# Layer A's gate as g (1 + tanh(g/2)) at its eviction, and two moves in the order of work

## The chip, the core and the metric

The kernel runs on one core of one Trainium2 chip. The metric is device time in microseconds for one execution; times before are of three runs. The engines in the profile are PE (TensorE matmuls; PEld its weight loads), DVE (VectorE), ACT (ScalarE), POOL (GpSimd) and SP (SyncE, whose queue issues all of the transfers here).

## The reference, cut to what matters

A decoder trunk of two layers on 2048 tokens of width 1024, in float32. Layer A makes q, k, v, forget logits and a gate from one normalized input, runs causal attention with a forget bias, multiplies by the gate's SiLU and projects. Layer B has its own gate and a windowed attention over shared keys that get a partial rotary.

```
u = rmsnorm(h, norm_a_g)
q, k, v, f_logit, gate = split(u @ w_in_a)
o = fox_attention(rmsnorm(q), rmsnorm(k), v, log_sigmoid(f_logit + b))   # exp(...) / sum
h = h + (o * silu(gate)) @ w_out_a
k_shared = partial_rope(rmsnorm((rmsnorm(h) @ w_kv)[:, :256]), positions)
...                                                                      # layer B
```

Since silu(g) = g sigmoid(g) = g (1 + tanh(g/2)) / 2, the gate can be carried without the half if something else is halved.

## The kernel before, in words

All large products are done as three float32r matmuls of split operands (high x high, high x low, low x high), 128 x 128 weights against 512 columns. The stages, by the profiled execution's clock:

- *Layer A's projections* (0 to 605 us): tokens in 16 blocks; `vectors` loads the small gain vectors in the first group, through `load_vectors` on SP's queue. `constants` makes `fold`, a 128 x 32 matrix of ones that sums partial rows.
- *Layer A's attention* (`attention_a`, 605 to about 1475 us): 320 steps, 20 for each of 16 heads. A step makes two blocks of scores in the three "sc" banks (L801, L802, masks L805), takes their exponential on ScalarE (L810, L814) into a tile of the tag "st" (four buffers), rounds it (L815, ScalarE), takes the low part (L816, GpSimd), adds it to the running sum in the one "ac" bank (L827, VectorE; started by L819, ended by the reduction L715), and multiplies by v three steps later (L842, "pa" bank, evicted by L850 into "sq"). Row maxima of queries 13 steps ahead run in the "mx" banks (L753; L764 and L769 on VectorE) and are stored as rows by small transfers (L430). `recips` sums the partial sums through `fold` (L724), takes the reciprocal (L729) and stores it to `rd`.
- *The gate in between.* `gate` is a generator that yields once per matmul (L872); `feed(n)` draws from it up to a total of n. The gate has 4 x 8 tiles of 128 rows x 512 tokens, 24 matmuls each. Each tile gathers in the one "pb" bank and reads its weights in two loads of 512 KB into "wr" (two buffers, L868); it is copied by ScalarE (L878) into "sq" and stored to `gt` (L879). `feed` is called at the end of each step, so that 28 of the 32 tiles (768 less `KEPT` = 96 matmuls) are spread over the 320 steps, 2.1 matmuls per step; the last four follow while the output weights are split (`half`, L360 and L361, through `between`).
- At step 125 `silus` loads the first 512 tokens' gate (all 1024 rows), takes Silu in two ScalarE instructions (L939) and stores it back. For these tokens `gated` (L1026 to L1032) runs at the end of attention, without Silu of its own.
- *Output projection* (`out_a`, about 1512 to 1695 us): four times 512 tokens. While one is multiplied (L1070), `gated_load` and `gated` prepare the next: attention's two parts are added (GpSimd, L1026), Silu of the gate (ScalarE, L1028), times 1/sum (L1029), times gate (L1030), split (L1031, L1032).
- *Layer B*, to the end. `rotary` (L277 to L280) makes four small products of the cosines and sines with the key gain `gk16`; they depend on that gain's load and on the buffer "rot", which the attention's mask holds until its last row maximum.

The order of instructions on each engine is not the program's order alone: a planner places each instruction by its own estimate of when operands and buffers are ready, and each engine then works through its list strictly in order. `keep_in_program_order` pins an instruction behind the one traced before it on its engine.

Of the kernel before, what the change touches and what calls it, by code (L numbers as in the profile page):

```python
# [3 lines left out]

# [1 line left out]

# [6 lines left out]
F32R = mybir.dt.float32r  # L13
BF16 = mybir.dt.bfloat16
I32 = mybir.dt.int32
AF = mybir.ActivationFunctionType
ALU = mybir.AluOpType
# [4 lines left out]
P = 128  # L22
# [3 lines left out]
NDT = D // P  # L26
# [17 lines left out]
PREP_AT = (284, 293, 304, 309, 314)  # L44

RAW_AT = 302

SILU_AT = 6 * 20 + 5

KEPT = 4 * 3 * NDT  # L50

# [37 lines left out]
class Trunk:  # L89
# [55 lines left out]
    def constants(self):  # L145
        nc, cp, a = self.nc, self.const, self.a

        def select(view, src, pattern, base, cm, fill):
            nc.gpsimd.affine_select(
                out=view, in_=src, pattern=pattern, compare_op=ALU.is_ge,  # L150
                fill=fill, base=base, channel_multiplier=cm,
            )

        def tile_(name, shape, dt=F32):
            return cp.tile(shape, dt, name=name, tag=name)

        self.ones = tile_("ones", [P, P])
        nc.gpsimd.memset(self.ones, 1.0)
        self.tri = tile_("tri", [P, P])
        select(self.tri, self.ones, [[1, P]], 0, -1, 0.0)  # L160
        self.ident = tile_("ident", [P, P])
        select(self.ident, self.tri, [[-1, P]], 0, 1, 0.0)

        self.fold = tile_("fold", [P, 32])
        nc.vector.tensor_tensor(self.fold, self.ident[:, :32], self.ident[:, 32:64], ALU.add)
        for c in (64, 96):
            nc.vector.tensor_tensor(self.fold, self.fold, self.ident[:, c : c + 32], ALU.add)
        self.identb = tile_("identb", [P, P], BF16)
        nc.vector.tensor_copy(self.identb, self.ident)

        self.mask_s = tile_("mask_s", [P, 2 * P], BF16)
        nc.gpsimd.memset(self.mask_s[:, :P], NEG)
        nc.gpsimd.memset(self.mask_s[:, P:], 0.0)
        select(self.mask_s[:, P:], self.mask_s[:, P:], [[1, P]], 0, -1, NEG)

        self.band = tile_("band", [P, 2, P], BF16)
        nc.gpsimd.memset(self.band, 0.0)
        select(self.band[:, 0, :], self.band[:, 0, :], [[1, P]], -1, -1, NEG)
        select(self.band[:, 1, :], self.band[:, 1, :], [[-1, P]], 0, 1, NEG)

        self.loads = []
        warm = tile_("warm", [P, 1])
        nc.scalar.activation(warm, self.ones[:, :1], AF.Sqrt)

        def vector(name, n, views):
            t = tile_(name, [P, n])
            for rows, src in views:
                self.loads.append((t[rows], src))
            return t

        def column(name, src, n):
            return vector(name, n, [(slice(0, P), src.rearrange("(t p) -> p t", p=P))])

        def pair_column(name, src):
            col = src.rearrange("(p o) -> p o", o=1)
            return vector(name, 1, [(slice(0, HD), col), (slice(HD, P), col)])

        def row(name, src, n):
            return vector(name, n, [(slice(0, P), src.to_broadcast([P, n]))])

        self.g_a = column("g_a", a["norm_a_g"][0], NDT)
        self.bf = row("bf", a["b_forget"], H)
        self.g_qa = pair_column("g_qa", a["qnorm_a_g"][0])
        self.g_ka = pair_column("g_ka", a["knorm_a_g"][0])
        self.g_b = column("g_b", a["norm_b_g"][0], NDT)
        self.g_kv = column("g_kv", a["kv_norm_g"], NDT)
        self.g_qb = pair_column("g_qb", a["qnorm_b_g"][0])
        self.g_kb = pair_column("g_kb", a["knorm_b_g"])
        self.sink = row("sink", a["sinks"], H)
        self.gq16 = row("gq16", a["qnorm_b_g"][:, :ROT], ROT)  # L210
        self.gk16 = row("gk16", a["knorm_b_g"].rearrange("(o d) -> o d", o=1)[:, :ROT], ROT)
        self.nsink = tile_("nsink", [P, H])

    def load_vectors(self, loads):
# [454 lines left out]
    def attention_a(self, w_out, result):  # L669
# [184 lines left out]

        def gate():

            for ch in range(NCH):
                us = []
                for dt in range(NDT):
                    us.append([self.sb(t, [P, CH], F32R) for t in ("wh", "wl")])  # L860
                    for k in range(2):
                        nc.sync.dma_start(out=f_(us[dt][k]), in_=d["ut"][ch, k, dt])
                for ft in range(NDT):
                    ps = self.ps("pb", [P, CH])
                    for dt in range(NDT):
                        if dt % 4 == 0:
                            w = self.sb("wr", [P, 2, 2, 2, P], F32R)
                            nc.sync.dma_start(  # L868
                                out=f_(w), in_=d["wg"][ft, :, dt // 2 : dt // 2 + 2]
                            )  # L870
                        for i, (wk, uk) in enumerate(((0, 0), (0, 1), (1, 0))):
                            nc.tensor.matmul(  # L872
                                ps, w[:, dt // 2 % 2, wk, dt % 2, :], us[dt][uk],
                                start=(dt == 0 and i == 0), stop=(dt == NDT - 1 and i == 2),
                            )
                            yield
                    g = self.sb("sq", [P, CH])
                    nc.scalar.copy(g, ps)  # L878
                    nc.sync.dma_start(  # L879
                        out=d["gt"][ft * P : (ft + 1) * P, ch * CH : (ch + 1) * CH], in_=g  # L880
                    )

        pieces, done, loaded = [], 0, 0

# [24 lines left out]
        yield  # L909
        pht, plt = self.sb("big", [P, 4, 1024], F32R), self.sb("big", [P, 4, 1024], F32R)  # L910
        filler, fed, total = gate(), 0, NCH * NDT * NDT * 3
        ready, prepared = [], 0
        Y = result

# [12 lines left out]

        def prepare():
            nonlocal prepared
            self.gated(prepared, Y, ready[prepared], silu=False)  # L930
            prepared += 1

        def silus():

            t = self.sb("big", [P, NDT, CH])
            gt = d["gt"][:, :CH].rearrange("(p r) t -> r p t", r=P)
            nc.sync.dma_start(out=t, in_=gt)
            for i in range(0, NDT, 4):
                nc.scalar.activation(t[:, i : i + 4], t[:, i : i + 4], AF.Silu)  # L939
            nc.sync.dma_start(out=gt, in_=t)  # L940

        def feed(n):
            nonlocal fed
            while fed < min(total, n):
                next(filler, None)
                fed += 1

        pending, due = [], []

        for n, (u, p) in enumerate(steps):  # L950
            h, ch = units[u]
            if n % per_head == LOAD_AT and h + 1 < H:
                more_pieces(len(pieces) + 1)
            target = per * (n + AHEAD + 1) // per_head + 1
            ahead(target - 1)
            pending.append(scores(n, u, p))
            ahead(target)
            if len(pending) > V_LAG:
                values(pending.pop(0))
            if p == 2 * ch + 1:  # L960
                if h == H - 1 and ch in (0, NCH - 1):
                    due.append((n + SUM_LAG, (h, ch and 1, ch + 1)))
                elif ch == NCH - 1:
                    due.append((n + SUM_LAG, (h,)))
            while due and due[0][0] <= n:
                recips(*due.pop(0)[1])
            feed((total - KEPT) * (n + 1) // len(steps))
            if n == SILU_AT:
                silus()
            if n == RAW_AT:  # L970
                raw = self.sb("big", [P, NDT, CH])
                for dt in range(0, NDT, 2):
                    nc.sync.dma_start(
                        out=raw[:, dt : dt + 2, :],
                        in_=w_out[dt * P : (dt + 2) * P, :CH].rearrange("(k p) c -> p k c", p=P),
                    )
            if n in PREP_AT:
                prepare_load()
                prepare()
        prepare_load()  # L980
        for item in pending:
            values(item)
            feed(fed + NDT)
# [34 lines left out]
                in_=d["rd"][h : h + 1, cols].to_broadcast([HD, CH]),  # L1018
            )

    def gated(self, p, Y, tiles, silu=True):

        nc = self.nc
        m, c, g, rb = tiles
        yh, yl = (Y[p // 4][:, k, p % 4, :] for k in range(2))
        nc.gpsimd.tensor_tensor(m, m, c, ALU.add)  # L1026
        if silu:
            nc.scalar.activation(g, g, AF.Silu)  # L1028
        nc.vector.tensor_tensor(m, m, rb, ALU.mult)  # L1029
        nc.vector.tensor_tensor(m, m, g, ALU.mult)  # L1030
        nc.scalar.copy(yh, m)  # L1031
# [6 lines left out]
    def out_a(self, w, res, dst, y, first, norm):  # L1038
# [3 lines left out]
        for ch in range(NCH):  # L1042
            more = ch + 1 < NCH
            after, tiles = None, []

            def load():
                mc, gr = self.sb("st", [P, 2, CH]), self.sb("wr", [P, 2, CH])
# [326 lines left out]
```

## Time and profile before

| | us |
|---|---|
| median of three runs | 2557.49 |
| the runs | 2551.67, 2557.49, 2557.59 |
| the profiled execution | 2549.98 |
| its span | 2548.2 |
| PE busy | 2486.3 |
| DVE busy | 1681.5 |
| ACT busy | 1360.4 |
| POOL busy | 941.2 |
| mean granted clock of PE | 0.992 |

The span runs from the first to the last instruction; 1.8 us of the execution lie around it. A row of a group gives line, engine, operation, output<-inputs and count, then total busy time and mean nanoseconds of one, then the idle time just before and who ended it. A row of the timeline gives start, duration, the same names, and in brackets how long the engine was idle before and what released it. A row of waits reads: who waited <- for whom: us in total, times, longest. The granted clock is 1.00 when the throttle lets TensorE run at full speed.

### The profile page before, as it was taken

To read this page: it belongs to the slowest core of one execution; us is meant where nothing else is said; L and a number is where in the kernel's file an instruction comes from. 1 tells how busy PE (TensorE), PEld (TensorE's weight loads), DVE (VectorE), ACT (ScalarE), POOL (GpSimd) and SP (SyncE) were. 2 spreads that over 40 slices of the span, in tenths; PEclk is the share of its full clock that TensorE was granted. 3 is DMA by queue.
4 is the path that set the end of the run, shared out by engine and by line. 5 is a ranking of instruction groups with operands and counts; after the bars stand their busy time and mean duration, and the time that the engine had idled before them with its cause. 6 is when DMAs were issued, how large, how long until landed. Compare 5 with 4: busy or idle time off the path is not lost.

```text
span 2548.2 us, 37618 instructions
## 1 busy us (share of the span) xinstructions
PE 2486.3 (98%) x12414; PEld 2070.7 (81%) x12414; DVE 1681.5 (66%) x4125; ACT 1360.4 (53%) x2645; POOL 941.2 (37%) x611
## 2 busy tenths in 40 slices
PE   8999999999999999999999889989999999899999
PEld 7888899987788778877887768767888888788887
DVE  5556556726888878888888954437756401688885
ACT  5423333415777787877777742224322213777774
POOL 0000000014877767877788822200011000355552
PEclk9999999999999999999999999999999999999999
DMA  5656545687454676565466578935434423756652
GB/s 190 181 154 189 163 147 162 195 264 217 136 161 118 187 207 170 158 179 157 118 172 193 164 213 264 285 121 157 125 101 115 141 83 120 193 158 163 172 142 66
DMA packets 357299, 420.34 MB, mean 165 GB/s; under 512 B 65105, under 2 KB 248401, under 8 KB 350929
## 3 DMA queue, kind: packets, MB, share of 16 engines
q1 hardware_dynamic: 357104, 417.94, 56.9%
q8 instruction: 98, 1.61, 0.3%
q14 instruction: 97, 0.79, 0.1%
HBM read 264.23 MB, written 153.49 MB: 164 GB/s over the span
## 4 chain that ended last, share of the span: by engine, by line
PE 84%; DMA 7%; DVE 4%; issue 2%; ACT 2%; SPq 1%; POOL 0%; DVEq 0%; ACTq 0%; POOLq 0%
PE b L584 29%; PE pa L842 10%; PE b L555 7%; PE pb L872 6%; PE pb L1216 6%; PE sc L801 5%; PE sc L802 5%; PE mx L753 5%; PE b L285 3%; PE pa L1181 2%; DMA wr<-rd 1%; PE b L1070 1%; PE b L1125 1%; PE b L1122 1%; PE pa L285 1%
## 5 line engine op out<-in xcount | busy, mean ns | idle before, releaser
L584 PE MATMUL b<-wh,big 128*128 128x512 f32 (+3 forms) x2560 | 775.0, 377 | 10.5 <-ACT wh L364 6.8
L816 POOL TENSOR_TENSOR big<-st,big 128x1024 fp32r<-128x1024 f32 (+1 forms) x320 | 680.6, 2138 | 248.7 <-ACT big L815 165.6
L584 PEld LDWEIGHTS b<-wh,big 128*128 128x128 f32 x2560 | 473.8, 189 | 81.7 <-ACT wh L364 8.9
L584 PE MATMUL b<-wl,big 128*128 128x512 f32 (+3 forms) x1280 | 476.3, 373 | 0.1
L827 DVE TENSOR_TENSOR ac<-ac,st 128x512 f32<-128x512 f32 (+3 forms) x576 | 354.6, 616 | 72.5 <-ACT st L810 29.5
L842 PE MATMUL pa<-big 128*128 128x512 f32 (+2 forms) x1280 | 331.4, 373 | 0.7 <-ACT sq L850 0.4
L810 ACT ACTIVATE st<-sc 128x512 f32<-128x512 f32 (+1 forms) x512 | 275.4, 585 | 101.9 <-PE sc L802 67.2
L815 ACT CAST big<-st 128x1024 fp32r<-128x1024 f32 (+1 forms) x320 | 302.5, 945 | 9.1 <-PE pa L842 1.2
L584 PEld LDWEIGHTS b<-wl,big 128*128 128x128 f32 x1280 | 243.2, 190 | 37.6 <-DVE wl L365 4.5
L842 PEld LDWEIGHTS pa<-big 128*128 128x128 f32 x1280 | 225.5, 191 | 40.9 <-ACT sq L850 7.9
L801 PE MATMUL sc<-big 128*128 128x512 f32 (+2 forms) x640 | 247.6, 387 | 5.4 <-ACT st L810 4.0
L764 DVE CUSTOM_DVE_ANT_0 mx<-mx,rot 128x128 f32<-128x128 f32 (+3 forms) x240 | 211.0, 879 | 47.8 <-PE mx L753 45.7
L377 ACT ACTIVATE sq<-b 128x512 f32<-128x512 f32 (+2 forms) x128 | 66.2, 518 | 322.6 <-PE b L584 318.2
L802 PE MATMUL sc<-big 67*128 67x512 f32 (+2 forms) x640 | 237.6, 371 | 0.0
L872 PE MATMUL pb<-wh,wr 128*128 128x512 f32 x512 | 191.4, 410 | 8.2 <-DMA wr<-wg 4.6
L753 PE MATMUL mx<-big 66*128 66x128 f32 (+3 forms) x660 | 192.7, 365 | 6.1 <-DVE mt L764 3.6
L379 DVE TENSOR_REDUCE sm<-sq 128x8 f32<-128x512 f32 (+2 forms) x128 | 74.9, 585 | 162.4 <-ACT sq L377 162.2
L1070 PE MATMUL b<-big 128*128 128x512 f32 x768 | 176.4, 391 | 4.4 <-DVE qn L1074 2.8
L1070 PEld LDWEIGHTS b<-big 128*128 128x128 f32 x768 | 143.6, 188 | 35.9 <-DVE qn L1074 3.4
L679 POOL MEMSET rot<- 128x1024 bf16 x1 | 1.0, 951 | 429.8 <-PE pb L285 429.8
L555 PE MATMUL b<-big,wh 128*128 128x512 f32 x512 | 158.7, 391 | 0.9 <-ACT st L561 0.9
L1151 POOL TENSOR_TENSOR st<-st,rs 128x1024 f32<-128x1024 f32 (+1 forms) x64 | 118.7, 1855 | 101.5 <-DVE rs L1150 87.4
(214 smaller groups left out, 4201.7 us busy)
## 6 DMA issues: line engine op xcount, KB each, us to landing
wr<-wg SPq DMA_DIRECT2D x64, 512.0 KB, 4.8
va<-st SPq DMA_DIRECT2D x32, 512.0 KB, 4.9
ka<-st SPq DMA_DIRECT2D x64, 256.0 KB, 3.8
ut<-big SPq DMA_DIRECT2D x16, 1024.0 KB, 5.9
big<-ka SPq DMA_DIRECT2D x16, 1024.0 KB, 5.4
big<-qa SPq DMA_DIRECT2D x16, 1024.0 KB, 5.6
qb<-st SPq DMA_DIRECT2D x64, 256.0 KB, 3.6
big<-qb SPq DMA_DIRECT2D x16, 1024.0 KB, 6.2
```

The costliest lines, as they stand in the source:

```text
L555: nc.tensor.matmul(ps, W[k][dt][:, ft * P : (ft + 1) * P], u[ch][:, dt, :], start=(dt == 0 and i == 0), stop=(dt == NDT - 1 and i == 2),)
L584: nc.tensor.matmul(ps[:, :n], u[tb // 4][:, dt, us], W[k][dt], start=(dt == 0 and i == 0), stop=(dt == NDT - 1 and i == 2),)
L753: mm = nc.tensor.matmul(ps[:, b, :wb], qb[:66, i * P : (i + 1) * P], kb[:66, k0 + b * wb : k0 + (b + 1) * wb], start=True, stop=True,)
L801: nc.tensor.matmul(o, ka[:, ks], qa[:, qs], start=not (last and n_), stop=False)
L802: nc.tensor.matmul(o, kb[:, ks], qb[:, qs], start=False, stop=not diag)
L810: nc.scalar.activation(pf[:, off : off + w], ps[:, :w], AF.Exp, scale=HD**-0.5)
L815: nc.scalar.copy(ph[:, :tw], pf[:, :tw])
L816: nc.gpsimd.tensor_tensor(pl[:, :tw], pf[:, :tw], f_(ph[:, :tw]), ALU.subtract)
L827: nc.vector.tensor_tensor(a_, a_, pf[:, off : off + w], ALU.add)
L842: nc.tensor.matmul(pv[:, q0 : q0 + w], v[:, k, :], src[:, off : off + w], start=(p == 0 and n_ == 0 and i == 0), stop=(last and n_ == 1 an ...
L872: nc.tensor.matmul(ps, w[:, dt // 2 % 2, wk, dt % 2, :], us[dt][uk], start=(dt == 0 and i == 0), stop=(dt == NDT - 1 and i == 2),)
L1070: nc.tensor.matmul(ps, y[p // 4][:, k, p % 4, ts_], W[nh][j][p], start=(p == 0 and i == 0), stop=(p == NDT - 1 and i == 2),)
```

## The change

The gate leaves its bank as g (1 + tanh(g/2)): ScalarE takes Tanh with a scale of 0.5 from the bank, and a VectorE operation adds one and multiplies by the bank. `fold` is doubled, so `recips` gives 1/(2 sum) and the product is the same. `silus` and the Silu in `gated` go away, for all four chunks of tokens.

`feed` gets a `pause`: in the steps it stops when a tile of the gate is complete, so that the next tile's first matmul is drawn in the next step. The generator now yields after a tile's last matmul only once its eviction and store are issued.

After the last step the gate's tiles gather in the "sc" banks instead of "pb", and their weight loads alternate between "st" and "wr".

The load of `gk16`, the last of `loads`, is taken out of `vectors` and issued in `out_a` before the second 512 tokens, so the keys' rotary factors can be made only after that.

```diff
+        nc.vector.tensor_single_scalar(self.fold, self.fold, 2.0, ALU.mult)
...
+        self.late = [self.loads.pop()]
...
-                    ps = self.ps("pb", [P, CH])
+                    ps = self.ps(gate_bank, [P, CH])
                     for dt in range(NDT):
                         if dt % 4 == 0:
-                            w = self.sb("wr", [P, 2, 2, 2, P], F32R)
+                            w = self.sb(next(weight_slots), [P, 2, 2, 2, P], F32R)
...
-                            yield
+                            if dt < NDT - 1 or i < 2:
+                                yield
                     g = self.sb("sq", [P, CH])
-                    nc.scalar.copy(g, ps)
+                    nc.scalar.activation(g, ps, AF.Tanh, scale=0.5)
+                    nc.vector.scalar_tensor_tensor(g, g, 1.0, ps, ALU.add, ALU.mult)
                     nc.sync.dma_start(
                         out=d["gt"][ft * P : (ft + 1) * P, ch * CH : (ch + 1) * CH], in_=g
                     )
+                    yield
...
         filler, fed, total = gate(), 0, NCH * NDT * NDT * 3
+        gate_bank, weight_slots = "pb", cycle(["wr"])
...
-        def silus():
-            t = self.sb("big", [P, NDT, CH])
-            gt = d["gt"][:, :CH].rearrange("(p r) t -> r p t", r=P)
-            nc.sync.dma_start(out=t, in_=gt)
-            for i in range(0, NDT, 4):
-                nc.scalar.activation(t[:, i : i + 4], t[:, i : i + 4], AF.Silu)
-            nc.sync.dma_start(out=gt, in_=t)
-
-        def feed(n):
+        def feed(n, pause=False):
             nonlocal fed
             while fed < min(total, n):
                 next(filler, None)
                 fed += 1
+                if pause and fed % (3 * NDT) == 0:
+                    break
...
-            feed((total - KEPT) * (n + 1) // len(steps))
-            if n == SILU_AT:
-                silus()
+            feed((total - KEPT) * (n + 1) // len(steps), pause=True)
...
         prepare_load()
+        gate_bank, weight_slots = "sc", cycle(["st", "wr"])
         for item in pending:
             values(item)
             feed(fed + NDT)
...
         nc.gpsimd.tensor_tensor(m, m, c, ALU.add)
-        if silu:
-            nc.scalar.activation(g, g, AF.Silu)
         nc.vector.tensor_tensor(m, m, rb, ALU.mult)
...
+            if ch == 1:
+                self.load_vectors(self.late)
```

More of the change, by code (lines that the diff above doesn't have):

```diff
@@ L3 @@
 from functools import partial
+from itertools import cycle
 import numpy as np
@@ L46 @@
 RAW_AT = 302
-SILU_AT = 6 * 20 + 5
 KEPT = 4 * 3 * NDT
@@ L929, in prepare @@
             nonlocal prepared
-            self.gated(prepared, Y, ready[prepared], silu=False)
+            self.gated(prepared, Y, ready[prepared])
             prepared += 1
-        def silus():
-            t = self.sb("big", [P, NDT, CH])
-            gt = d["gt"][:, :CH].rearrange("(p r) t -> r p t", r=P)
-            nc.sync.dma_start(out=t, in_=gt)
-            for i in range(0, NDT, 4):
-                nc.scalar.activation(t[:, i : i + 4], t[:, i : i + 4], AF.Silu)
-            nc.sync.dma_start(out=gt, in_=t)
-        def feed(n):
+        def feed(n, pause=False):
             nonlocal fed
@@ L1019, in gated_load, with gated @@
             )
-    def gated(self, p, Y, tiles, silu=True):
+    def gated(self, p, Y, tiles):
         nc = self.nc
```

## The prediction

> **What bounds the kernel now.** I read the page first, then busy time by stage, then the stretches in which TensorE was not full. The page gives the bound:
>
> ```profile
> span 2548.2 us, 37618 instructions
> PE 2486.3 (98%) x12414; PEld 2070.7 (81%) x12414; DVE 1681.5 (66%) x4125; ACT 1360.4 (53%) x2645; POOL 941.2 (37%) x611
> ```
>
> TensorE works 98% of the span, and the change removes none of its matmuls. So it can gain only TensorE's idle time and the time at a lowered clock; both are found by stage (columns: stretch, length, busy time by engine, then granted clock, DMA share, GB/s):
>
> ```profile
> 605.00:900.00 295.00, 294.81 (x1453) 236.20 (x1453) 243.84 (x453) 235.89 (x370) 235.38 (x112) 1.00 0.57 163
> 900.00:1000.00 100.00, 97.62 (x458) 76.38 (x458) 77.67 (x138) 79.45 (x118) 71.49 (x34) 0.97 0.66 190
> 1000.00:1340.00 340.00, 339.82 (x1670) 273.46 (x1669) 285.65 (x531) 268.74 (x417) 266.84 (x127) 1.00 0.57 158
> 1340.00:1440.00 100.00, 95.47 (x461) 76.11 (x460) 89.09 (x149) 74.78 (x117) 82.32 (x40) 0.98 0.66 186
> 1512.00:1700.00 188.00, 179.44 (x802) 147.16 (x800) 86.95 (x144) 45.29 (x74) 31.21 (x24) 1.00 0.80 241
> ```
>
> Layer A's attention (605 to 1475) runs TensorE without a gap for 295 and again for 340 us. Its losses sit in four places, quoted next. For each I count idle time (length minus PE busy) plus busy time times (1 minus the granted clock):
>
> ```profile
> 928.00:956.00 28.00, 25.79 (x104) 18.59 (x102) 18.80 (x36) 25.43 (x35) 15.01 (x7) 0.88 0.72 217
> 1398.00:1410.00 12.00, 9.04 (x36) 6.89 (x35) 10.74 (x14) 7.42 (x11) 9.87 (x5) 0.86 0.64 187
> 1454.00:1466.00 12.00, 8.02 (x25) 6.20 (x24) 9.27 (x15) 7.48 (x12) 9.53 (x5) 0.72 0.61 177
> 1478.00:1510.00 32.00, 24.27 (x87) 18.18 (x86) 15.02 (x23) 9.69 (x18) 1.95 (x2) 0.84 0.82 244
> ```
>
> That is 2.2 + 3.1 = 5.3 us; 3.0 + 1.3 = 4.3 us; 4.0 + 2.2 = 6.2 us; 7.7 + 3.9 = 11.6 us. The change touches what stands in the first, third and fourth place.
>
> **Part 1, the separate Silu pass goes (L939).**
>
> ```profile
> L939 ACT ACT_TABLE_LOAD  x2: 1283/1283/1283, 928.6 to 939.8; - x2
> L939 ACT ACTIVATE big<-big x2: 1916/1916/1917, 929.9 to 941.1; 128x2048 f32<-128x2048 f32 x2
> L810 ACT ACT_TABLE_LOAD x3 | 3.8, 1283 | 0.1
> big<-gt SPq DMA_DIRECT2D x1, 2048.0 KB, 9.8
> 933.90 0.50 PE L753 MATMUL mx<-big 66*128 66x512 f32 x1 [0.85 <-DVE mt L764]
> ```
>
> Each half of the pass puts 1.28 (its table) + 1.92 + 1.28 (Exp's table again) = 4.48 us ahead of the exponentials, so ScalarE was busy 25.4 of 28 us there, scores came late, and TensorE met waits such as the 0.85 us. All 5.3 us go: **-5.3**. Its 2 MB load and 2 MB store go too; no wait of TensorE there is put down to a transfer, so 0.
>
> The lowered clock in that stretch came although its longest quoted gap is 0.85 us. The Trainium skill ("TensorE: Matmul & The Clock Gate", Part 1) says the clock halves after an idle window of about 3.4 us; by that rule these gaps would not have lowered it, the dips would stay after the change, and the sum below would lose its clock terms. The row of 928 to 956, at 0.88 with 2.2 us idle in pieces, speaks against that threshold; the 295 us without a gap stand at 1.00.
>
> **Part 2, the keys' rotary factors move (L277 to L280, and their gain's load).** Now they run on VectorE beside a busy GpSimd:
>
> ```profile
> L277 DVE TENSOR_TENSOR rot<-cossin,gq x2: 283/284/285, 1819.8 to 1915.9; 128x128 f32<-128x128 f32 x2
> L277 DVE TENSOR_TENSOR rot<-cossin,gk x1: 1891/1891/1891, 1442.5 to 1442.5; 128x128 f32<-128x128 f32 x1
> L278 DVE TENSOR_TENSOR rot<-cossin,gk x1: 1889/1889/1889, 1445.0 to 1445.0; 128x128 f32<-128x128 f32 x1
> L279 DVE SCALAR_TENSOR_TENSOR rot<-cossin,gk x1: 1886/1886/1886, 1447.4 to 1447.4; 128x128 f32<-128x128 f32 x1
> L280 DVE TENSOR_TENSOR rot<-cossin,gk x1: 774/774/774, 1452.3 to 1452.3; 128x128 f32<-128x128 f32 x1
> 1457.22 0.59 ACT L819 COPY ac<-st 128x512 f32<-128x512 f32 x1 [5.06 <-DVE part L715]
> 1458.39 0.80 PE L801 MATMUL sc<-big 128*128 128x512 f32 x1 [3.98 <-ACT st L810]
> ```
>
> The four take 1.89 + 1.89 + 1.89 + 0.77 = 6.44 us where the same form takes 0.28 later. The accumulator's sum (L715) ends late behind them, ScalarE waits 5.06 us for it in order, and TensorE 3.98 us for ScalarE. 6.44 exceeds 5.06, so with the four gone the wait goes: **-6.2**. What could be late next is the long work beside it (L1029, L1030), which stays; it would come back in part if a gate tile's new operation fell there.
> In the output projection they cost 4 x 0.28 = 1.1 us of a VectorE that is busy 87 of 188 us, and one 0.43 us issue on SP's queue ahead of the second 512 tokens' loads, which are followed by TensorE within the same stage: **+1.0** for both and for transfers crowded by the earlier start (ends: 0, and 2 us, the 1.9 us that TensorE now waits there up to 1660):
>
> ```profile
> L217 SPq DMA_DIRECT2D gk<-in_knorm_b_g x1: 429/429/429, 67.3 to 67.3; - x1
> PE b L1070 <- ACT big L1031: 1.6, 2, 1.1
> PE b L1070 <- DVE qn L1074: 0.3, 1, 0.3
> L1028 ACT ACTIVATE wr<-wr 128x512 f32<-128x512 f32 x24 | 15.2, 632 | 54.7 <-DMA wr<-gt 32.9 <-DMA h<-qn 17.7 <-DMA wr<-rd 3.4
> ```
>
> The 24 Silus (L1028) also leave that stage. ScalarE is busy 45 of 188 us there, so this is worth 0.
>
> **Part 3, the last four gate tiles get the three score banks, and "st" beside "wr" for weights.**
>
> ```profile
> PE pb L872 <- DMA wr<-wg: 4.3, 4, 2.1
> PE pb L872 <- ACT sq L878: 3.4, 1, 3.4
> wr<-wg SPq DMA_DIRECT2D x64, 512.0 KB, 4.8
> ```
>
> One load lands after 4.8 us and feeds 12 matmuls, 2.7 us at the projection's spacing (179.44 us / 802 = 0.22); with two buffers TensorE must wait, 4.3 us in all between 1475 and 1512, and 3.4 us on the only bank. With three banks and up to six buffers both waits go, and the slow clock behind them: -11.6. Three things come back. "st" is held by exponentials until GpSimd is done with them, so the first loads may land late (one such wait was 2.1); the last tiles now leave by two engines instead of one, and the projection's first tile may need their bank (0.59 + 0.74, rows below); and 32 us at 244 GB/s squeezed into some 23 would be 340, so not all loads come in time, though the output weights' second half can wait. I put back 3: **-8.6** (ends: -11.6, and 0 if the loads bound it).
>
> **Part 4, the eviction in attention.** A ScalarE copy becomes a Tanh of the same size, followed by a VectorE operation with one PSUM and one SBUF operand, 28 times in attention.
>
> ```profile
> L878 ACT COPY sq<-pb 128x512 f32<-128x512 f32 x32 | 18.8, 587 | 6.1 <-PE pb L872 5.8 <-DMA wr<-wg 0.3
> L406 DVE SCALAR_TENSOR_TENSOR st<-pa,g_ka,st 128x512 fp32r<-128x512 f32 x16 | 11.9, 745 | 2.5 <-ACT st L405 2.4
> L827 DVE TENSOR_TENSOR ac<-ac,st 128x512 f32<-128x512 f32 x384 | 271.5, 707 | 60.1 <-ACT st L810 29.5 <-ACT ac L819 20.9
> L1029 DVE TENSOR_TENSOR qn<-qn,wl 128x512 f32<-128x512 f32 x7 | 11.3, 1619 | 2.5 <-POOL qn L1026 1.2 <-DMA wl<-rd 1.2
> 605.00:1475.00 870.00, 727.47 (x1307) 0.99 0.59 165
> ```
>
> Tanh for Copy: 0 on ScalarE. The new operation is between 0.71 us (L827, PSUM and SBUF, beside the busy GpSimd) and 1.62 us (L1029, two SBUF operands beside it). I take 0.745, L406, the same operation on the same kinds of operands. 28 x 0.745 = 21 us on a VectorE busy 727 of 870 us. On TensorE's path this is between 0 (VectorE has 143 us idle) and 21 us (each in full). Queued behind it on VectorE are the row maxima and the accumulations, and those matmuls that need their banks wait for them; "pb" comes free later by that operation, and so do the "sq" buffer and the store on SP's queue, which the next maxima rows and weights follow. The pause covers the bank: a tile ends once in 870 / 28 = 31 us and the next begins a step (870 / 320 = 2.7 us) later, against 0.59 + 0.745 = 1.3 us. I take 0.1 us per tile, **+3.0**, near the low end, because 635 us of attention show TensorE full at the present VectorE load.
>
> No row has a Tanh; if it needed a table of its own, each tile would pay two loads (rival 3). The Trainium skill ("ScalarE: Activation LUTs", Table sets: the hidden batching unit) lists tanh in exp's set, which would make it 0; no run here shows it yet.
>
> **Part 5, the doubled fold matrix**: one small VectorE operation before the first matmuls, **+0.1**. One load fewer early on SP: 0.
>
> **The sum:** -5.3 - 6.2 + 1.0 - 8.6 + 3.0 + 0.1 = -16.0 us. The profiled execution took 2549.98, so 2534. The runs' median of 2557.49 is 7.5 above that execution; the forecast on that scale is 2541.
>
> **The rivals.**
> 1. *The tail's gain is given back.* The tail already moves 244 GB/s and the projection 241; if transfers bind, TensorE finishes the gate early and waits in the projection. For it: DMA share 0.82 and 0.80. Against: TensorE waits only 1.9 us there. Without the 8.6: 2550.
> 2. *VectorE becomes the bound of attention (the slower side).* The new operation waits in order for the Tanh, which waits behind exponentials; what is queued behind it delays TensorE at each of 28 tiles. At x us per tile the result is 2538 + 28x: 2557 at 0.7, slower by over 0.3% from 0.97 on. For it: the 3.98 us wait above is just such a chain. Against: a sixth of VectorE's time is free.
> 3. *Tanh switches tables.* Silu's 9 us of extra ScalarE time cost 5.3; two loads, 2.57 us, would cost 1.5 per tile, 42 us: 2583. Nothing in the trace excludes it.
> 4. *A wait takes another's place near 1454* (L1029 and L1030 still run there): without the 6.2, 2547.
> 5. *The clock's dips do not come from these gaps* and stay: the gains shrink by 3.1 + 2.2 + 3.9 = 9.2, to 2550. Against: the quoted stages show dips only next to gaps. This is where the clock rule of the Trainium skill weighed in part 1 would lead for the short gaps.
>
> **How the numbers follow.** Under 0.3% (7.7 us) counts as no change, so faster means below 2549.8, slower above 2565.2. Forecast 0.54 (all but 0.01 faster); rival 1 0.14 and rival 5 0.04 (both half faster, half same); rival 2 0.17 (0.02 faster, 0.06 same, 0.09 slower); rival 3 0.04 (slower); rival 4 0.07 (0.05 faster, 0.02 same). Together 0.69, 0.18, 0.13. The low end, 2527, is the whole 23.1 us at no cost (2534) less 7 for a run like the quickest; the high end, 2557, takes in rivals 1, 4, 5 and half of 2.
>
> **What would show it.** Right: no Silu pass and no table loads in attention; TensorE full around step 125; L277 to L280 at 0.28 us in the output projection and no 4 us wait before 1458; no waits of the last four gate tiles on their bank, and the projection starting some 20 us earlier; the new operation at 0.7 us. Wrong: table loads at each gate tile, matmuls of the maxima waiting longer on VectorE, or waits on loads in the projection that were not there.

## The result, and the profile after

The changed kernel takes 2537.88 us (median of 6 runs, 2531.38 to 2542.9) against 2554.81 us (median of 6 runs) for the kernel before: a ratio of 0.9932, 95% interval 0.9916 to 0.9948, 16.9 us. Measured a second time, the ratio was 0.9937 (0.9923 to 0.9952). Its profiled execution took 2537.57 us, 12.4 less than that of before (2549.98). Lines of the attention stand 2 to 4 higher in this kernel (L872 is now L875, L868 is L871, L879 is L884, L430 is L432). In the experiments the numbers shift by a few lines more.

The page:

```profile
span 2535.7 us, 37563 instructions
PE 2477.2 (98%) x12414; PEld 2065.3 (81%) x12414; DVE 1693.9 (67%) x4158; ACT 1335.0 (53%) x2614; POOL 941.3 (37%) x611
```

VectorE has 12.4 us more to do, ScalarE 25.4 less. The view by stage (stretch, length, busy time by engine, granted clock, DMA share, GB/s), with the stretches of the prediction:

```profile
605.00:900.00 295.00, 292.44 (x1443) 234.90 (x1444) 246.18 (x457) 234.24 (x368) 232.83 (x111) 1.00 0.58 163
900.00:1000.00 100.00, 99.43 (x489) 80.18 (x489) 84.79 (x156) 77.12 (x121) 76.33 (x38) 1.00 0.59 167
1000.00:1340.00 340.00, 337.82 (x1661) 273.26 (x1660) 289.52 (x535) 266.40 (x414) 266.45 (x126) 0.99 0.55 154
1340.00:1440.00 100.00, 96.04 (x468) 75.91 (x467) 92.78 (x153) 76.58 (x120) 84.40 (x41) 1.00 0.65 189
1440.00:1475.00 35.00, 31.65 (x132) 24.11 (x131) 30.21 (x39) 26.73 (x45) 30.84 (x15) 0.90 0.47 130
1475.00:1500.00 25.00, 20.83 (x91) 16.27 (x90) 11.79 (x20) 7.73 (x14) 0.00 (x0) 1.00 0.85 261
...
928.00:956.00 28.00, 28.00 (x139) 22.40 (x138) 24.95 (x49) 22.42 (x36) 22.54 (x12) 1.00 0.56 144
1454.00:1466.00 12.00, 12.00 (x58) 9.29 (x57) 9.52 (x12) 11.37 (x19) 11.81 (x7) 1.00 0.28 89
```

The holes at 928 and at 1454 are closed. But the two stretches that TensorE had filled before (605 to 900, 1000 to 1340) now have 2.6 and 2.2 us of idle time. The projection (L1071) starts at 1500.7 instead of 1512.1 and lasts 181.9 instead of 182.4 us; Layer B is 0.6 us shorter. So nearly all of the gain lies before the projection's first matmul.

The next table is worked out from many rows of that view, in slices of 2 us: idle time of TensorE plus its busy time times (1 minus the granted clock), in us. Four kernels are in it; the last two come from the experiments below. The losses explain most of each start, not all: part of a wait is hidden in the modelled ends of matmuls.

| stretch | before | changed | later store | old handover |
|---|---|---|---|---|
| 605–925 | 0.4 | 2.6 | 0.5 | 0.0 |
| 925–960 | 5.6 | 0.6 | 0.0 | 0.0 |
| 960–1350 | 0.2 | 4.3 | 0.7 | 1.0 |
| 1350–1440 | 6.2 | 3.5 | 4.5 | 8.4 |
| 1440–1475 | 7.1 | 6.3 | 8.6 | 4.8 |
| 1475–projection | 12.1 | 4.2 | 1.4 | 2.8 |
| projection starts at | 1512.1 | 1500.7 | 1492.2 | 1494.9 |

Who TensorE waited for in the changed kernel, in 605 to 1340, then in 1340 to 1475, then in 1475 to 1500:

```profile
PE pb L875 <- DMA wr<-wg: 5.2, 4, 2.2
PE sc L803 <- DVE st L425: 1.4, 1, 1.4
...
PE pa L844 <- POOL big L818: 2.0, 3, 1.3
PE mx L755 <- DVE mt L766: 1.5, 3, 0.6
PE pb L875 <- DVE sq L883: 1.4, 1, 1.4
...
PE sc L875 <- DMA st<-wg: 3.0, 2, 1.6
PE sc L875 <- DMA wr<-wg: 1.2, 1, 1.2
```

The first row is new. The wait for the gate's weights was 0.3 us in the same stretch before, and is 5.2 us now. (The second is attention's first matmul, at 605.0; in the kernel before that matmul waited 1.40 us too, for a load, just ahead of this stretch.) The timeline of the changed kernel shows one of its four places, first on VectorE:

```profile
728.03 0.69 DVE L883 SCALAR_TENSOR_TENSOR sq<-sq,pb 128x512 f32<-128x512 f32 x1
```

on SP's queue:

```profile
723.55 0.59 SPq L704 DMA_DIRECT2D big<-qa  x1
728.75 0.33 SPq L884 DMA_DIRECT2D gt<-sq  x1
729.12 3.37 SPq L432 DMA_DIRECT2D big<-m  x4
...
733.82 2.54 SPq L432 DMA_DIRECT2D big<-m  x4
736.46 0.54 SPq L871 DMA_DIRECT2D wr<-wg  x1
```

and on TensorE:

```profile
740.77 0.50 PE L875 MATMUL pb<-wh,wr 128*128 128x512 f32 x1 [1.42 <-DMA wr<-wg]
```

The same place on SP's queue in the kernel before:

```profile
725.33 2.44 SPq L430 DMA_DIRECT2D big<-m  x4
727.87 0.54 SPq L879 DMA_DIRECT2D gt<-sq  x1
...
731.05 2.49 SPq L430 DMA_DIRECT2D big<-m  x4
733.63 0.54 SPq L868 DMA_DIRECT2D wr<-wg  x1
```

Before, the four row stores of a maximum (L430) went out from 725.33 on, and the gate's store behind them. Now the gate's store stands ahead of them in SP's list. It waits for the new VectorE operation, which ends at 728.72, and SP issues nothing from 724.1 to 728.75. The four row stores follow, then two stores of attention's output and four more row stores, and so the weight load goes out at 736.46, 2.8 us later than before; its data come 4.3 us after that, and TensorE waits 1.42 us.

### The profile page after: what moved, and what is told of

It reads as the page before. It is cut to its first block, busy times and chain, and to the rows that moved or that the text cites. A ratio compares the mean times of both kernels' runs of the same rounds, so it can differ in the third digit from the quotient of the medians.

```text
span 2535.7 us, 37563 instructions
## 1 busy us (share of the span) xinstructions
PE 2477.2 (98%) x12414; PEld 2065.3 (81%) x12414; DVE 1693.9 (67%) x4158; ACT 1335.0 (53%) x2614; POOL 941.3 (37%) x611
## 4 chain that ended last, share of the span: by engine, by line
PE 84%; DMA 7%; DVE 4%; ACT 2%; issue 2%; SPq 1%; POOL 1%; DVEq 0%; ACTq 0%; POOLq 0%
PE b L586 30%; PE pa L844 9%; PE b L557 7%; PE pb L1217 6%; PE pb L875 6%; PE sc L803 5%; PE mx L755 5%; PE sc L804 5%; PE b L287 3%; DMA wr<-rd 3%; PE b L1071 2%; PE pa L1182 2%; PE b L1126 1%; PE b L1123 1%; PE pb L287 1%
## 5 line engine op out<-in xcount | busy, mean ns | idle before, releaser
L1071 PE MATMUL b<-big 128*128 128x512 f32 x768 | 177.6, 391 | 2.9 <-DVE qn L1075 1.8
L875 PE MATMUL pb<-wh,wr 128*128 128x512 f32 x448 | 166.2, 401 | 7.1 <-DMA wr<-wg 5.2
L1071 PEld LDWEIGHTS b<-big 128*128 128x128 f32 x768 | 143.1, 188 | 36.0 <-DVE qn L1075 3.9
```

The costliest lines, as they stand in the source:

```text
L875: nc.tensor.matmul(ps, w[:, dt // 2 % 2, wk, dt % 2, :], us[dt][uk], start=(dt == 0 and i == 0), stop=(dt == NDT - 1 and i == 2),)
L1071: nc.tensor.matmul(ps, y[p // 4][:, k, p % 4, ts_], W[nh][j][p], start=(p == 0 and i == 0), stop=(p == NDT - 1 and i == 2),)
```

## The experiments

Each kernel was timed against the kernel before on the same chip; the ratios below are to that. The runs were made in three groups (the first four, the next four and the last four), each on another chip, so kernels of two groups are compared by their ratios alone. What tells theories apart is above all where TensorE waits in the trace, since single executions of one kernel differ by 5 to 10 us.

**One part alone: the Silu pass taken out of the kernel before.**

```diff
-            if n == SILU_AT:
-                silus()
```

> The kernel before without the call of silus, part 1 of the change alone; it leaves out the Silu of the first 512 tokens' gate. My step: the loss of 5.3 us around step 125 goes, the rest of the trace stays, so about 5 us faster than before (ratio 0.998). Rival, that the lowered clock there does not come from the gaps: about 2 us faster, with a clock below 1 still around 940 to 955 us.

2545.7 us, ratio 0.9975 (0.9965 to 0.9985): 6.4 us. The stretch of the pass:

```profile
928.00:956.00 28.00, 28.00 (x138) 22.06 (x137) 23.82 (x46) 23.27 (x37) 21.45 (x11) 1.00 0.52 147
```

Idle time and clock dip went together, with nothing else changed: both hung on the pass. Its transfers went with it (DMA share 0.52 instead of 0.72), so this run does not separate them from its time on ScalarE.

**One part alone: the keys' gain loaded late (rotary factors in the projection).**

```diff
+        self.late = [self.loads.pop()]
...
+            if ch == 1:
+                self.load_vectors(self.late)
```

> The kernel before with the key gain loaded in the output projection, part 2 alone. My step: the keys' rotary products leave attention, the 4 us wait before 1458 us and its slow clock go, 1 us comes back: 5 us faster. Rival, drawn from the trace after the change, which still loses about 6 us between 1440 and 1475: another wait takes the place of this one, and the gain is 1 us or less.

2552.12 us, ratio 0.9991 (0.9981 to 1.0001): 2.3 us, not told from nothing. In the trace, the projection starts 5.0 us earlier (1507.1), but that execution (2545.26) was nearly the quickest of its eleven. The stretch is better but not whole:

```profile
1440.00:1475.00 35.00, 32.16 (x146) 24.13 (x144) 30.22 (x37) 29.94 (x50) 34.79 (x16) 1.00 0.52 154
```

The loss there falls from 7.1 to 2.85 us; a 1.5 us wait for GpSimd's low parts is among the waits that come in its place.

**One part alone: three banks and two kinds of weight buffers for the last four tiles.**

```diff
-                    ps = self.ps("pb", [P, CH])
+                    ps = self.ps(gate_bank, [P, CH])
...
-                            w = self.sb("wr", [P, 2, 2, 2, P], F32R)
+                            w = self.sb(next(weight_slots), [P, 2, 2, 2, P], F32R)
...
+        gate_bank, weight_slots = "sc", cycle(["st", "wr"])
```

> The kernel before with the three score banks and the st and wr buffers for the last four gate tiles, part 3 alone. My step: 8 to 9 us faster, no wait on the gate's bank between 1475 and 1512 and fewer waits on loads, the output projection starting 8 to 9 us earlier. Rival, that the gain is given back in the projection: its matmuls wait 5 us or more longer than before, and the whole is 0 to 3 us faster.

2546.85 us, ratio 0.9972 (0.9961 to 0.9984): 7.2 us, near the 8 to 9 expected. But the projection starts only 3.8 us earlier (1508.3), not 8 to 9; the rest of the gain stands in the projection itself, which takes 178.3 instead of 182.4 us. Its first matmul waits for the eviction of a gate tile from a shared bank, as the prediction had feared:

```profile
PE b L1073 <- ACT sq L879: 2.7, 1, 2.7
```

The three parts alone give 6.4 + 2.3 + 7.2 = 15.9 us, about what the whole change gives. If the parts simply added, that would leave the new eviction near nothing net, although the table shows a new loss at it. The next runs go after that.

**One part undone: the changed kernel with the keys' gain loaded early again.**

```diff
-        self.late = [self.loads.pop()]
+        self.late = []
```

> The changed kernel with the key gain loaded early again, so part 2 alone is undone. My step: 5 us slower than the changed kernel, 12 us faster than the kernel before (ratio 0.995), with a loss between 1440 and 1475 us above the 6.3 us of the changed kernel by 5. Rival: the changed kernel's other waits hide it, and it is within 1 us of the changed kernel (ratio 0.993).

2539.2 us, ratio 0.9943 (0.993 to 0.9957), not told from the changed kernel; in the profiled execution the projection starts 2.85 us later (1503.5). The waits of TensorE in 1440 to 1475:

```profile
PE pb L875 <- DVE sq L883: 3.4, 1, 3.4
PE pa L844 <- POOL big L818: 3.1, 4, 1.3
```

What VectorE does ahead of the first of them, with the first of the four products:

```profile
1436.12 2.50 DVE L279 TENSOR_TENSOR rot<-cossin,gk 128x128 f32<-128x128 f32 x1
1438.54 2.86 DVE L1029 TENSOR_TENSOR qn<-qn 128x512 f32<-128x512 f32 x1
```

Three of the four products are long again (2.50, 2.39 and 1.60 us; the fourth takes 0.28), but what waits is another: the gate's bank, for the new VectorE operation, which stands behind the first product and L1029. In the changed kernel, with L1029 alone in front, that wait is 1.4 us. By this execution's start the move is worth about 3 us in the company of the other parts; the medians cannot tell it from nothing.

**The eviction without Tanh and VectorE.**

```diff
-                    nc.scalar.activation(g, ps, AF.Tanh, scale=0.5)
-                    nc.vector.scalar_tensor_tensor(g, g, 1.0, ps, ALU.add, ALU.mult)
+                    nc.scalar.copy(g, ps)
```

> The changed kernel with the eviction as the plain ScalarE copy of before, so the price of part 4 alone is taken away; it leaves out the gate's tanh and product. My step (0.1 us per tile): 3 us faster than the changed kernel. Theory from its trace, that the store of each gate tile now waits for VectorE on SP's queue and holds up the row maxima and the weight loads behind it: the four waits of gate matmuls on weight loads (5.2 us, with 1.7 us of slow clock) go, so 5 to 8 us faster than the changed kernel, ratio to before 0.990 to 0.991. Rival, that the pause causes those waits: they stay.

2538.48 us, ratio 0.9934 (0.9922 to 0.9946): no faster than the changed kernel, as far as these runs can tell (some 5 us). Both forecasts missed, the 3 us by the operation's price and the 5 to 8 us by SP's order. Its wait for weights in 605 to 1340 is still 1.7 us, and its gate store still stands ahead of the row stores (store 727.21, rows 727.63). What it saves there is lost again in 1350 to 1475 (12.5 us, against 9.8).

**A second VectorE operation at each gate tile, which leaves the output as it is.**

```diff
                     nc.vector.scalar_tensor_tensor(g, g, 1.0, ps, ALU.add, ALU.mult)
+                    nc.vector.scalar_tensor_tensor(g, ps, 0.0, g, ALU.mult, ALU.add)
```

> The changed kernel with a second VectorE operation of the same size behind each gate tile's eviction (it adds zero times the bank, the output is unchanged). If VectorE's load or the chain behind the eviction sets the price, each tile costs about as much again: by my step 3 us more than the changed kernel, by the slower rival (0.7 us per tile) 20 us more. If the price is only a matter of the order on SP's queue, 0 to 3 us more.

2532.64 us, ratio 0.991 (0.9895 to 0.9924): more work on VectorE, and faster if anything, which no forecast had. The wait for weights in 605 to 1340 is nearly gone:

```profile
PE sc L803 <- ACT st L812: 0.7, 3, 0.2
PE pb L875 <- DMA wr<-wg: 0.3, 1, 0.3
```

In this program three of the four row stores stand ahead of the gate's store (rows from 724.32, store 728.24), and the weight load leaves at 733.56; the planner presumably allowed for the longer chain. That fits the theory of SP's order; a load on VectorE alone cannot explain it.

**The pause taken out of the changed kernel.**

```diff
-            feed((total - KEPT) * (n + 1) // len(steps), pause=True)
+            feed((total - KEPT) * (n + 1) // len(steps))
```

> The changed kernel without the pause. By my step the pause covers the bank's later release: without it the next tile's first matmul waits for Tanh and the VectorE operation, up to 1.3 us at 28 tiles, so 0 to 36 us slower, I take 10 us slower, with waits on the bank in the trace. Rival, that the pause delays the weight loads: the waits on weight loads go, 3 to 5 us faster.

2540.19 us, ratio 0.9941 (0.9928 to 0.9953), where 10 us slower had been expected: no difference that these runs can tell. The store still stands ahead of the row stores (730.07, rows from 730.44), and the wait for weights is 2.8 us.

**The gate's store issued after the third matmul of the next tile.**

```diff
+                            if held and dt * 3 + i == 2:
+                                store()
...
-                    nc.sync.dma_start(
-                        out=d["gt"][ft * P : (ft + 1) * P, ch * CH : (ch + 1) * CH], in_=g
-                    )
+                    held.append((g, ft, ch))
+                    if fed >= total - KEPT - 1:
+                        store()
```

> The changed kernel with the store of each of the 28 gate tiles issued after the third matmul of the next tile, otherwise the same. By the theory of SP's queue the store no longer waits there for VectorE ahead of the row maxima and weight loads, and the waits on weight loads in attention (5.2 us and 1.7 us of slow clock) go or shrink: 3 to 7 us faster than the changed kernel. If the loads are late for another reason, the waits stay and the time is that of the changed kernel within 2 us.

2530.04 us, ratio 0.9902 (0.9889 to 0.9915): the fastest of all, 25 us faster than before and, by the ratios, some 8 faster than the changed kernel. SP's queue at the same place (three of its rows):

```profile
724.46 2.44 SPq L432 DMA_DIRECT2D big<-m  x4
727.18 0.35 SPq L861 DMA_DIRECT2D gt<-sq  x1
...
732.97 0.54 SPq L879 DMA_DIRECT2D wr<-wg  x1
```

TensorE's waits in 605 to 1340, in full:

```profile
PE pb L883 <- DMA wr<-wg: 1.0, 2, 0.5
```

The row stores go first, the weight load leaves at 732.97 instead of 736.46, and the wait falls from 5.2 to 1.0 us. The new operation is still there, 28 times.

**The new eviction alone, in the kernel before without the Silu pass.**

```diff
-                    nc.scalar.copy(g, ps)
+                    nc.scalar.activation(g, ps, AF.Tanh, scale=0.5)
+                    nc.vector.scalar_tensor_tensor(g, g, 1.0, ps, ALU.add, ALU.mult)
...
-            if n == SILU_AT:
-                silus()
```

> The kernel before without the Silu pass, and with the new eviction (Tanh on ScalarE, then the VectorE operation) at its old place between the tiles; sums are not doubled and the late sigmoid factor is not put right, so the gate's values differ from the reference's, and nothing in the timing does. In this program each gate store stands behind the four row stores of the maxima (big<-m) as in the kernel before, with 4 row stores between it and the next weight load at the tiles where the changed kernel has 8. Theory S (the price of part 4 in attention is the order of SP's queue: the store ahead of row stores and weight loads, so that weight loads come late): no price here, the same as without the Silu pass alone, ratio to before 0.9975 within 0.0012 (2545 to 2551), and waits of TensorE for weights in 605 to 1340 of at most 2 us. Theory V (the price is the load that 28 operations put on VectorE): 3 to 6 us slower than without the Silu pass alone, ratio 0.9985 to 1.0.

2554.9 us, ratio 1.0005 (0.9995 to 1.0016): 7.7 us (about 4 to 11) slower than without the pass alone. By the number, this speaks against the theory of SP's order and for a price of the operation itself, even above the forecast 3 to 6; by the trace, the loss isn't in steady attention. The stage view of 605 to 1340:

```profile
605.00:1340.00 735.00, 734.72 (x3626) 594.09 (x3626) 628.31 (x1160) 584.02 (x913) 584.74 (x277) 1.00 0.57 163
```

The gate's waits on TensorE in 605 to 1340, then the longest in 1340 to 1510:

```profile
PE pb L872 <- DMA wr<-wg: 0.2, 1, 0.2
...
PE pb L872 <- DVE sq L879: 10.2, 3, 4.9
```

With the row stores ahead of the gate's store (723.50, store 726.22), 735 us of attention run without a loss, new operation and all. The price stands at the end, where VectorE is late and the one bank waits for it: 10.2 us in three waits, the longest 4.9 (without the new eviction, one wait of 3.8 for the copy). Yet the projection starts at 1507.4, only 0.8 us later than without the pass alone; it takes 192 us there, with 7.4 us of waits for VectorE to empty its banks. So part of this price shows in the projection. Why it does isn't settled: the profiled execution without the pass alone had such waits too (7.0 us), and was one of the slowest of its eleven. So the parts do not add: with this loss, the four alone would give 8.2 us, and together they give 16.9.

**Later store and second operation together.**

> The changed kernel with the gate tile's store issued after the third matmul of the next tile, and with a second VectorE operation (0.67 us) at each of the 32 tiles that leaves the output as it is. Theory S: the load of 28 x 0.67 = 19 us on VectorE costs nothing in attention; the time is that of the later store alone, 2530, within 4 us, unless the added operation moves the row stores again. Theory V: 3 to 6 us slower than the later store alone, 2533 to 2536 or more; and if the gain of the second operation and that of the later store were two different things, they would add: 2525.

2537.4 us, ratio 0.993 (0.9915 to 0.9946). The profiled execution, the fastest of its six (2531.96), has 1.0 us of waits for weights and a start at 1496.6. So the operation that seemed to gain 5 us costs 7 here by the medians, across two chips. That is a miss for the theory of SP's order, which had 2530 within 4 us, and what the theory of VectorE's load had forecast. Steady attention shows no place for it: 605 to 1340 loses 1.8 us in all. Against the later store alone, the projection starts 4.4 us later in the profiled execution, and 2.2 us of it are in the waits for the last four tiles' weights (5.6 us against 3.4), most of them in 1475 to 1512 on the tag "st":

```profile
PE sc L883 <- DMA st<-wg: 4.5, 2, 3.1
```

How the operation would lengthen these stays open, and so does where the medians' other microseconds go, since the trace is that of the quickest execution.

**The handover at a tile's end as before (the yield after the last matmul, no pause).**

```diff
-                            if dt < NDT - 1 or i < 2:
-                                yield
+                            yield
...
                         out=d["gt"][ft * P : (ft + 1) * P, ch * CH : (ch + 1) * CH], in_=g
                     )
-                    yield
...
-            feed((total - KEPT) * (n + 1) // len(steps), pause=True)
+            feed((total - KEPT) * (n + 1) // len(steps))
```

> The changed kernel with the handover at a tile's end as in the kernel before: the feeding pauses after the tile's last matmul, not after its store, and without the added pause. In this program each store stands behind the row stores again (4 between it and the next weight load at the tiles where the changed kernel has 8). Theory S: 6 to 9 us faster than the changed kernel, 2529 to 2533; waits of TensorE for weights in 605 to 1340 fall from 5.2 us to below 1.5. Rival B (the bank): the next tile's first matmul stands right behind the eviction on the same bank, which takes ScalarE and VectorE 0.60 + 0.67 us; if that shows, 0.3 to 0.7 us per tile is lost, 28 x 0.5 = 14, 2545 or more.

2533.93 us, ratio 0.9924 (0.9907 to 0.9941), beside the changed kernel's 2537.3: 3.4 us, within the scatter and short of the 6 to 9 forecast. The trace shows the mechanism, on SP's queue:

```profile
724.55 2.44 SPq L432 DMA_DIRECT2D big<-m  x4
727.27 0.35 SPq L883 DMA_DIRECT2D gt<-sq  x1
...
733.03 0.54 SPq L871 DMA_DIRECT2D wr<-wg  x1
```

and TensorE's waits in 605 to 1340, in full:

```profile
PE pb L875 <- DMA wr<-wg: 0.5, 2, 0.3
```

The order of before is back and the wait is nearly gone. Without the pause alone the order was still that of the changed kernel; so it is the moved yield, which issues eviction and store together with a tile's last matmul, that put the store ahead of the row stores. The late weights need both the moved yield and the longer eviction: TensorE waits 2.8 to 5.2 us for weights in 605 to 1340 with both (0.3 with the second operation, where the order came out otherwise), 1.7 with the copy and the moved yield, 0.2 and 0.5 with the new eviction and the old yield, 0.3 and 1.5 with neither (before, and without the Silu pass). Of the 6.5 us won between 605 and 1350, 4.9 are given back in 1350 to 1440, where the changed kernel loses 3.5 and this one 8.4. One wait of 2.3 us there is on the gate's bank, for the new operation; a maxima bank is waited for 3.0 us at a time.

**The changed kernel again, beside the last three.**

> The changed kernel once more, beside the three others on the same chip, so that they are held against it directly. Every theory: ratio to before 0.992 to 0.995, 2535 to 2542; weight loads late at the same places (waits of TensorE for weights in 605 to 1340 of 4 to 6 us).

2537.3 us, ratio 0.9937 (0.9923 to 0.9952); weights late by 4.1 us at four places.

## Why the prediction was right, and where its steps were not

The forecast of 2541 us stood 16.5 below the median then known; 16.9 was measured. On the scale of the profiled executions it was 2534, and 2537.57 came: 3.6 us of the 16.0 are missing. Against the median of all six runs before, 2554.81, the forecast stood 13.8 below.

**Part 1** (-5.3): right. The loss in 925 to 960 fell by 5.0 us, alone by 5.6, and by 6.4 in the medians. Rival 5 is out for this place: the dip went when its short gaps (the 0.85 us among them) went. The changed kernel shows the same with a single gap, at the late weights of 1173 (two slices of the stage view):

```profile
1173.00:1176.00 3.00, 2.94 (x9) 2.33 (x10) 1.50 (x3) 0.15 (x1) 2.16 (x1) 0.65 0.75 276
1176.00:1180.00 4.00, 4.00 (x18) 3.31 (x17) 2.22 (x4) 2.14 (x3) 0.17 (x1) 0.84 0.60 169
```

and the matmul behind the gap, in the timeline:

```profile
1173.06 0.50 PE L875 MATMUL pb<-wh,wr 128*128 128x512 f32 x1 [2.18 <-DMA wr<-wg]
```

After 2.18 us of idle time the clock was 0.65, then 0.84. But 4.2 us of idle time in pieces of up to 1.6 us between 1475 and 1500 stood at 1.00. So in this trace short gaps could lower it and need not. The Trainium skill ("TensorE: Matmul & The Clock Gate", Part 1) puts the window at about 3.4 us and calls it free-running; a window that need not be wholly idle would fit both rows, a threshold of 3.4 us of idle time does not fit the first.

**Part 2** (-6.2 and +1.0): the step that failed. The 4 us wait is gone and the four products take 0.285 us each in the projection, as predicted:

```profile
L281 DVE SCALAR_TENSOR_TENSOR rot<-cossin,gk x1: 285/285/285, 1552.2 to 1552.2; 128x128 f32<-128x128 f32 x1
```

But the loss in 1440 to 1475 fell only from 7.1 to 6.3. The prediction's "6.44 exceeds 5.06, so with the four gone the wait goes" is true of that wait only; others take its place (GpSimd's low parts, 2.0 us; the gate's bank, 1.4). The second is what part 2 and rival 4 had warned of, long work beside GpSimd with a gate tile's operation behind it:

```profile
1438.52 2.78 DVE L1029 TENSOR_TENSOR qn<-qn 128x512 f32<-128x512 f32 x1
1443.29 0.61 PE L875 MATMUL pb<-wh,wr 128*128 128x512 f32 x1 [1.39 <-DVE sq L883]
```

Alone the move gave 5.0 us at the projection's start and 2.3 in the medians, in company about 3 at the start. The +1.0 did not show: the projection became 0.5 us shorter.

**Part 3** (-8.6): right in size, and half right in its way there. The tail's loss fell from 12.1 to 4.2 us, by 7.9; alone it was 7.2 in the medians. No wait for a bank is left in the changed kernel, and the clock stays at 1.00. But of "both waits go" only the bank's is true: TensorE still waits 4.2 us for weights, where it waited 4.3, more than the 3 put back. Rival 1 did not come: the projection did not slow down. "Some 20 us earlier" for the projection's start was too much; it was 11.4.

**Part 4** (+3.0): the right sign, twice the size, and for another reason. On ScalarE nothing was added, and rival 3 is out. Table loads, and the new pair:

```profile
L812 ACT ACT_TABLE_LOAD x1 | 1.3, 1283 | 0.0
L883 DVE SCALAR_TENSOR_TENSOR sq<-sq,pb 128x512 f32<-128x512 f32 x28 | 18.9, 674 | 0.4 <-ACT sq L882 0.3
L882 ACT ACTIVATE sq<-pb 128x512 f32<-128x512 f32 x28 | 16.7, 597 | 3.1 <-PE pb L875 3.1
```

One table load is left in attention, at its start, and none belongs to the Tanh. The operation takes 0.674 us, where 0.745 was taken. But "0.1 us per tile" spread over 28 tiles is not what happened. The cost was 6.4 us in 605 to 925 and 960 to 1350 together, nearly all of it in waits for weights and the slow clock behind them: the store "which the next maxima rows and weights follow" was named in the prediction and given no price of its own. Its price came from the moved yield, which the prediction read only as a pause that covers the bank. In 1350 to 1440, where the prediction had no term, the loss fell by 2.7 us; what helps there is not shown. The run with the old handover lost 8.4, but the run with the plain copy lost 7.6 with the new handover.

So -5.0 - 0.8 - 7.9 + 6.4 - 2.7 = -10.0 us of losses, against a start 11.4 us earlier. That the total came so near is luck in part, because the misses had both signs: part 2 gave 5.4 us less than its 6.2 and part 4 cost 3.4 more than its 3.0, while 1350 to 1440 gave 2.7 and the projection 0.5 that the sum did not have, and its +1.0 did not come. Rival 2 did not come in steady attention; where VectorE is late, at the end, the new operation does hold the bank, 10.2 us with one bank and no pause. What the operation costs by itself is not settled: two runs (the eviction alone, and the second operation on the later store) were some 7 us slower for it, and two (the plain copy, and the second operation) say otherwise.

## What to carry to other kernels

Here the place of an instruction that waits in SP's list counted more than its length: a store of 0.33 us that waited for a computed value, listed ahead of small stores and of the load that TensorE needed next, delayed them all. When a change regroups what is issued in one step, list each queue's order before and after around that step, and price the latest load behind it. And a wait that goes is worth only its excess over the next one at the same place: run the parts alone and in company.

## What was not expected

- A second operation of 0.68 us on a VectorE that is 84% busy (620 of 735 us) came with a faster kernel (0.991 against 0.9932 and 0.9937), with SP's queue ordered otherwise by the planner; with the order already mended, the same operation came with 2537.4 instead of 2530 us. Additions on this kernel cannot be priced one at a time.
- Three of the four small products took 1.89 us each beside a busy GpSimd, and 0.285 where GpSimd works 32 of 200 us, while the new operation, with one operand in PSUM, kept 0.674 us beside a GpSimd that is busy 78% of the time. The Trainium skill ("SBUF — State Buffer", SBUF: two separate sides) says that a VectorE operation with two SBUF inputs and a GpSimd operation lock each other out of a shared port; these durations agree with it.
